# Transposes of q and k in the first attention block: from TensorE to a trip through HBM and VectorE's 32x32 blocks

## The chip, the cores and the metric

The kernel runs on one core of one Trainium2 chip. The time is device time in microseconds of one execution; 1035.2 us is the median of three runs of the kernel before (1035.12, 1035.2 and 1038.44 us). A profile is one execution recorded by the hardware profiler; that of the kernel before took 1035.85 us, of which 1034.1 us lie between its first and its last instruction (the span). Engines are named as in the profile: PE is the matmul engine (PEld its weight loads), DVE the VectorE, ACT the ScalarE, POOL the GpSimd, SP the SyncE, which here only issues DMAs.

## The reference

One decoder layer over 256 tokens of width 2048, all float32. What matters here is its first attention group:

```
h = rmsnorm(x)
[A.q | A.k | A.v | B.c_q | B.c_kv | B.k_rope] = h @ w_in          # 2048 x 4160
A: 8 heads x 128; rotary on the first 32 channels of q and k
   scores = q k^T * 128^-0.5 + mask (three dilated windows, merged)
   out    = softmax(scores) v
B: latent attention, 8 heads, from c_q, c_kv, k_rope
x = x + rmsnorm(concat(A, B) @ w_out);  x = x + rmsnorm(relu(rmsnorm(x) @ w_up)^2 @ w_down)
```

The three dilated windows of the reference, weighted by their softmax denominators, come to one softmax over 256 keys with a bias that holds the logarithm of how many windows a key lies in; the kernel computes them so.

## The kernel before, in words

The 256 tokens are two blocks of 128 (`b` = 0, 1). A matmul of this kernel in float32r is made of three passes (`hi` by `hi`, `lo` by `hi`, `hi` by `lo`), where ACT writes `hi` as a rounded copy of a weight tile (line 311) and DVE the rest `lo` (line 312). A weight tile `raw` comes by a DMA from SP (line 195); five `raw` and eight `hi`/`lo` buffers let this work run some six tiles ahead of PE. One tile of a 512 wide projection feeds 12 matmuls of 512 columns (two k blocks, two token blocks, three passes).

The order of every engine's instructions is written by the program itself: a small planner (`Flow`) holds a clock that each matmul moves on by its estimated cost, and chains (Python generators) that are resumed when the clock has passed the delay that they last yielded. What a chain issues goes into the queues between the matmuls of the projection that runs just then. Engines work through their queues in order, and semaphores are added by the framework, so a chain that is resumed too early makes its engine wait, and whatever stands behind it on that engine.

The first attention group runs in two halves of four heads. For half 0 one projection gives q and k together (`acc_qk`, 192 matmuls), then v (`acc_v`, 96). For half 1 there are three projections of 96 matmuls each: `acc_q`, `acc_k`, `acc_v`. Behind each projection a chain `evac_a` scales the PSUM sums into an SBUF tile `q`, `k` or `v` of 128 tokens x 512 channels per token block (ACT, line 675; the scale `rstd_pre` comes from POOL, line 506), and turns the first 32 channels of each head of q and k by their rotary tables (`rope`, DVE, lines 615 to 618).

When the three chains of a half have ended, `heads_a` starts the four heads in two chains of two heads (0, 1 and 2, 3). For a head it has four PE transposes of 128x128 (q and k, two token blocks; `qkT_a`, line 305) into one PSUM bank, a DVE copy of 128x512 out of it (line 661), then two score matmuls (`sc_a`, line 301), and then `softmax_pv`: bias and maximum on DVE (line 626), exponentials on ACT (line 632), normalising on DVE (lines 635 and 637), three PE transposes of the probabilities (`pT_a`) with an ACT copy (line 643), and the product with v (`o_a`), which ACT and DVE split into the `hi` and `lo` parts of `mixT` (lines 311 and 312). The heads of half 0 run between the matmuls of half 1's projections, those of half 1 between the matmuls of the two projections that follow, `acc_ckv` (192 matmuls of 288 columns) and `acc_cq` (96 of 512).

PSUM has eight banks: four for projections, two for transposes (`tp_bank`, taken in turn by `qkT_a`, `pT_a`, `ckvt` and all later ones), and two for attention (`at_bank`, taken in turn by `sc_a` and `o_a`). Behind `acc_ckv` the chain `latent` transposes the latent `ckv` in two steps of four transposes (`ckvt`), each of which ACT and DVE split out of its bank (lines 315 and 316).

Later in the kernel the result of the up projection is transposed by a trip through HBM and VectorE already: a DMA from ACT's queue writes it out in rows of 512 bytes (`rkeep`, line 965), another reads it back (line 978), and DVE transposes 32x32 blocks (line 980).

Of the kernel before, what the change touches and what calls it, by code (L numbers as in the profile page):

```python
# [18 lines left out]
F32 = mybir.dt.float32  # L19
# [3 lines left out]
AF = mybir.ActivationFunctionType  # L23
# [3 lines left out]
P = 128  # L27
D = 2048
S = 256
NB = S // P  # L30
# [5 lines left out]
RA = 32  # L36
# [51 lines left out]
DA = (3.0, 0.5, 3.0, 3.0, 4.0, 3.0, 0.5)  # L88
# [40 lines left out]
MM = 512 / 2400 + 0.0025  # L129
# [139 lines left out]
def layer(nc, tc, io):  # L269
    flow = Flow()  # L270
# [8 lines left out]
    dram = tc.alloc_tile_pool(name="dram", bufs=1, space=bass.MemoryType.DRAM)  # L279
# [13 lines left out]
    def tp_bank(name):  # L293
        return next_bank(4, 2, name)
# [5 lines left out]
    def mm(out, a, b, start, stop, cost=MM):  # L300
        nc.tensor.matmul(out, a, b, start=start, stop=stop)  # L301
        flow.spend(cost)

    def transpose(out, a):
        nc.tensor.transpose(out, a, ident)
        flow.spend(TR)
# [140 lines left out]
    for c in range(2):  # L447
        wide_d.append([])
        for what, k in DOWN_STEPS[c]:
            if what == "k":  # L450
                ts = [weights.plan(down_weight(c, k), 1, CW)]
            else:
                q, parts_q, back = [lambda c=c, k=k, f=f: f(c, k) for f in (down_sums, down_split, down_back)]
# [57 lines left out]
    pa = pool("pa", "right")  # L511
# [50 lines left out]
    rstd0 = []  # L562
# [19 lines left out]
    def tables():  # L582

        yield D_TAB[0]
        nc.scalar.dma_start(out=pos_i, in_=io["pos"])
        nc.scalar.dma_start(out=cst, in_=io["consts"])
        yield D_TAB[1]
        pos_f = con.tile([P, NB], F32, name="pos_f")
        nc.vector.tensor_copy(pos_f, pos_i)
        ang = pa.tile([P, 2, NB, 96], F32, tag="qkT", bufs=2, name="ang")  # L590
        kk_ = pa.tile([P, 2, NB, 96], F32, tag="qkT", bufs=2, name="kk_")
        for w in range(2):
            for b in range(NB):
                nc.vector.tensor_scalar_mul(ang[:, w, b, :], freq[:, w * 96:(w + 1) * 96], pos_f[:, b:b + 1])
            nc.vector.tensor_scalar(kk_[:, w], ang[:, w], 1.0 / (2 * np.pi), 0.25 * w, op0=OP.mult, op1=OP.add)
        yield 1.0
        nc.vector.tensor_scalar(kk_, kk_, MAGIC, -MAGIC, op0=OP.add, op1=OP.add)
        for c in (C1, C2, C3):
            nc.vector.scalar_tensor_tensor(out=ang, in0=kk_, scalar=-c, in1=ang, op0=OP.mult, op1=OP.add)
        yield 1.0  # L600
        nc.vector.tensor_scalar_add(ang[:, 1], ang[:, 1], float(np.pi / 2))
        nc.vector.tensor_scalar(ang, ang, PI_LO, -PI_LO, op0=OP.min, op1=OP.max)
        yield 4.0
        nc.scalar.activation(trig, ang, AF.Sin)
# [43 lines left out]
        split(mixT[0][:, head, :], mixT[1][:, head, :], o[:, :S])  # L648


    def heads_a(qkv, half, hs, after):
        while any(c in flow.chains for c in after):
            yield 0.5
        for h in hs:
            nm = f"a{half}{h}"
            tp = tp_bank(f"qkT_{nm}")
            for i, w in enumerate("qk"):
                for b in range(NB):
                    transpose(tp[:, (2 * i + b) * P:(2 * i + b + 1) * P], qkv[w][:, b, h * 128:(h + 1) * 128])
            qkT = pa.tile([P, 512], F32, tag="qkT", bufs=2, name=f"qkT_{nm}")  # L660
            nc.vector.tensor_copy(qkT, tp)
            yield DA[0]
            sc = at_bank(f"sc_{nm}")
            mm(sc[:, 0:128], qkT[:, 0:128], qkT[:, 256:384], True, True, MM)
            mm(sc[:, 128:384], qkT[:, 128:256], qkT[:, 256:512], True, True, 2 * MM)
            yield DA[1]
            yield from softmax_pv(pa, DA, sc, bias_a, SCALE_A,
                                  [qkv["v"][:, b, h * 128:(h + 1) * 128] for b in range(NB)], half * 4 + h, nm)
            yield DA[6]

    def evac_a(t, accs, nm, half):
        while pre in flow.chains:
            yield 0.5
        for b in range(NB):
            nc.scalar.activation(t[:, b, :], accs[b][0], AF.Copy, scale=rstd0[0][:, b:b + 1])
        yield 1.0
        while tab in flow.chains:
            yield 0.5
        if nm != "v":
            tv = t.rearrange("p b (h d) -> p b h d", d=128)[:, :, :, :RA]  # L680
            rope(pa, tv, tv, RA // 2, 4, 0, f"{nm}{half}")

    pre = flow.start(prelude())
    tab = flow.start(tables())
# [1 line left out]
    for half in range(2):  # L686
        qkv = {}
        for nms in (("qk", "v") if not half else "qkv"):
            accs = [acc for _, _, acc in proj(xT, [ch_a[half, nms]], f"{nms}{half}",
                                              bank_of=at_bank if (half, nms) == (0, "v") else None)]  # L690
            for i, nm in enumerate(nms):
                t = pa.tile([P, NB, 512], F32, tag=nm, name=f"{nm}_{half}")
                qkv[nm] = t
                evacs.append(flow.start(evac_a(t, [[acc[i]] for acc in accs], nm, half)))
            flow.pump()
        flow.finish(*heads)
        heads = [flow.start(heads_a(qkv, half, hs, evacs), 2.0 + d) for hs, d in (((0, 1), 0.0), ((2, 3), D_PAIR))]
# [58 lines left out]
    kT = pb.tile([P, HB, S], F32, name="kT")  # L756
# [634 lines left out]
```

## Time and profile before

| | |
|---|---|
| median of 3 runs | 1035.2 us |
| the profiled execution | 1035.85 us, span 1034.1 us |
| PE busy | 1022.4 us (99%) |
| DVE, ACT, POOL busy | 834.4 us (81%), 634.6 us (61%), 63.5 us (6%) |
| mean DMA rate | 245 GB/s |
| granted TensorE clock | 0.997 |

Busy time says how much an engine does, the chain of work that ended last says which engine the end waited for. In rows of the timeline and of the chain the first number is the start in us from the span's start and the second the time taken; xN is the number of instructions in the row. In groups, the numbers behind the bar are the busy time in us and the mean ns of one instruction. In rows of DMA issues the last number is the median time in us from the issue to the landing of the data.

### The profile page before, as it was taken

To read this page: it belongs to the slowest core of one execution; us is meant where nothing else is said; L and a number is where in the kernel's file an instruction comes from. 1 tells how busy PE (TensorE), PEld (TensorE's weight loads), DVE (VectorE), ACT (ScalarE), POOL (GpSimd) and SP (SyncE) were. 2 spreads that over 40 slices of the span, in tenths; PEclk is the share of its full clock that TensorE was granted. 3 is DMA by queue.
4 is the path that set the end of the run, shared out by engine and by line. 5 is a ranking of instruction groups with operands and counts; after the bars stand their busy time and mean duration, and the time that the engine had idled before them with its cause. 6 is when DMAs were issued, how large, how long until landed. Compare 5 with 4: busy or idle time off the path is not lost.

```text
span 1034.1 us, 13262 instructions
## 1 busy us (share of the span) xinstructions
PE 1022.4 (99%) x4718; PEld 851.3 (82%) x4718; DVE 834.4 (81%) x1125; ACT 634.6 (61%) x850; POOL 63.5 (6%) x100
## 2 busy tenths in 40 slices
PE   9999999999999999999999999999999999999996
PEld 6888889889888878888888888888888888888885
DVE  6675536577547669999999999898999999899795
ACT  6585536566446467666775767666666665767571
POOL 0000000000001010000100100000101000211100
PEclk9999999999999999999999999999999999999998
DMA  8975447554438478877989887589989867888962
GB/s 288 361 237 166 138 136 223 155 163 144 144 122 263 142 276 284 272 239 258 285 258 302 269 262 258 191 275 335 354 267 366 299 240 258 302 314 303 329 240 82
DMA packets 105298, 253.44 MB, mean 245 GB/s; under 512 B 8720, under 2 KB 29712, under 8 KB 104848
## 3 DMA queue, kind: packets, MB, share of 16 engines
q1 hardware_dynamic: 65744, 175.14, 50.8%
q0 software_dynamic: 16112, 57.68, 16.8%
q10 hardware_dynamic: 23376, 19.78, 6.1%
q8 instruction: 37, 0.61, 0.2%
q14 instruction: 29, 0.24, 0.1%
HBM read 224.78 MB, written 27.79 MB: 244 GB/s over the span
## 4 chain that ended last, share of the span: by engine, by line
PE 96%; DVE 1%; DMA 1%; issue 1%; ACT 0%; POOL 0%; DVEq 0%; POOLq 0%; SPq 0%; ACTq 0%
PE acc_u L301 26%; PE y L301 25%; PE acc_o L301 8%; PE md L301 6%; PE m L301 6%; PE acc_v L301 4%; PE acc_qk L301 4%; PE acc_ckv L301 2%; PE acc_ukv L301 2%; PE acc_q L301 2%; PE acc_cq L301 2%; PE acc_k L301 2%; PE acc_uq L301 2%; PE sc_b L301 1%; DMA raw<-in_w_in 1%
## 5 line engine op out<-in xcount | busy, mean ns | idle before, releaser
L312 DVE TENSOR_TENSOR lo<-raw,hi 128x1024 fp32r<-128x1024 f32 (+3 forms) x207 | 234.1, 1149 | 83.9 <-ACT hi L311 82.5
L311 ACT ACTIVATE hi<-raw 128x1024 fp32r<-128x1024 f32 (+3 forms) x207 | 203.4, 996 | 70.9 <-DMA raw<-in_w_in 16.8
L301 PE MATMUL acc_u<-hi,hT_lo 128*128 128x512 f32 x386 | 150.3, 389 | 0.4 <-DVE hT_lo L312 0.4
L301 PE MATMUL acc_u<-hi,hT_hi 128*128 128x512 f32 x386 | 150.7, 390 | 0.0
L301 PE MATMUL acc_u<-lo,hT_hi 128*128 128x512 f32 x386 | 150.2, 389 | 0.0
L301 PE MATMUL y<-hi,uhi 128*128 128x512 f32 x358 | 139.3, 389 | 0.0
L301 PE MATMUL y<-lo,uhi 128*128 128x512 f32 x358 | 139.3, 389 | 0.0
L301 PE MATMUL y<-hi,ulo 128*128 128x512 f32 x358 | 139.3, 389 | 0.0
L315 ACT ACTIVATE hi<-raw,gcol 128x1024 fp32r<-128x1024 f32 x86 | 97.0, 1148 | 33.1 <-PE acc_u L301 18.2
L316 DVE SCALAR_TENSOR_TENSOR lo<-raw,gcol,hi 128x1024 fp32r<-128x1024 f32 x86 | 106.7, 1273 | 9.4 <-ACT hi L315 9.3
L301 PEld LDWEIGHTS acc_u<-hi,hT_lo 128*128 128x128 f32 x386 | 72.5, 188 | 15.9 <-DVE hT_lo L312 0.8
L301 PEld LDWEIGHTS acc_u<-lo,hT_hi 128*128 128x128 f32 x386 | 72.5, 188 | 14.9
L301 PEld LDWEIGHTS acc_u<-hi,hT_hi 128*128 128x128 f32 x386 | 72.5, 188 | 14.7
L301 PEld LDWEIGHTS y<-hi,uhi 128*128 128x128 f32 x358 | 67.2, 188 | 14.1
L301 PEld LDWEIGHTS y<-lo,uhi 128*128 128x128 f32 x358 | 67.2, 188 | 13.9
L301 PEld LDWEIGHTS y<-hi,ulo 128*128 128x128 f32 x358 | 67.2, 188 | 13.9
L312 DVE TENSOR_TENSOR lo<-st_down,hi 128x1024 fp32r<-128x1024 f32 x46 | 55.0, 1219 | 0.6 <-ACT hi L311 0.6
L301 PE MATMUL acc_o<-hi,mixT_hi 128*128 128x512 f32 x128 | 51.8, 405 | 0.0
L311 ACT ACTIVATE hi<-u 128x1024 fp32r<-128x1024 f32 (+1 forms) x33 | 32.2, 979 | 29.7 <-PE acc_u L301 11.7
L301 PE MATMUL acc_o<-hi,mixT_lo 128*128 128x512 f32 x128 | 50.2, 392 | 0.0
L301 PE MATMUL acc_o<-lo,mixT_hi 128*128 128x512 f32 x128 | 50.0, 390 | 0.0
L311 ACT ACTIVATE hi<-st_down 128x1024 fp32r<-128x1024 f32 x46 | 47.8, 1049 | 3.5 <-DVE st_down L371 2.1
(338 smaller groups left out, 2018.9 us busy)
## 6 DMA issues: line engine op xcount, KB each, us to landing
raw<-in_w_up SPq DMA_DIRECT2D x86, 512.0 KB, 4.8
raw<-in_w_down SPq DMA_DIRECT2D x82, 512.0 KB, 6.1
raw<-in_w_in SPq DMA_DIRECT2D x55, 512.0 KB, 5.1
ab<-in_w_up POOLq DMA_DIRECT2D x17, 1024.0 KB, 7.4
raw<-in_w_out SPq DMA_DIRECT2D x32, 512.0 KB, 4.4
ab_down<-in_w_down POOLq DMA_DIRECT2D x11, 1024.0 KB, 8.9
ulo<-ukeep POOLq DMA_DIRECT2D x20, 512.0 KB, 6.4
rkeep<-r ACTq DMA_DIRECT2D x28, 256.0 KB, 3.4
```

The lines of the kernel that those rows point to most:

```text
L301: nc.tensor.matmul(out, a, b, start=start, stop=stop)
L311: nc.scalar.activation(hi, src, AF.Copy)
L312: nc.vector.tensor_tensor(out=lo, in0=src, in1=hi.bitcast(F32), op=OP.subtract)
L315: nc.scalar.activation(hi, src, AF.Copy, scale=g)
L316: nc.vector.scalar_tensor_tensor(out=lo, in0=src, scalar=g, in1=hi.bitcast(F32), op0=OP.mult, op1=OP.subtract)
```

## The change

The transposes `qkT_a` and the copies out of PSUM are gone. The tiles `q` and `k` get a third block of 512 columns: the projection is now evacuated into blocks 1 and 2, with the channels reordered so that channels 0 to 31 of the four heads come first, then channels 32 to 63, and so on (`a h c` in place of `h a c`). Behind the rotary step, `evac_a` issues from POOL two DMAs that write the two blocks to HBM in rows of 512 bytes (`keep`), after 5 us of the planner's clock two that read them back, and after 8 us more DVE transposes each block in 32x32 pieces (`nc.vector.transpose`), from block 1 to block 0 and from block 2 to block 1. Blocks 0 and 1 then hold the channels of each head on the partitions and the tokens along the row, so the score matmuls read them in place. The tile of half 1 is not taken before the four heads of half 0 have issued their scores (`scored`). The tables' two scratch tiles move to another tag.

```
-            tp = tp_bank(f"qkT_{nm}")
-            for i, w in enumerate("qk"):
-                for b in range(NB):
-                    transpose(tp[:, (2 * i + b) * P:(2 * i + b + 1) * P], qkv[w][:, b, h * 128:(h + 1) * 128])
-            qkT = pa.tile([P, 512], F32, tag="qkT", bufs=2, name=f"qkT_{nm}")
-            nc.vector.tensor_copy(qkT, tp)
-            yield DA[0]
+            qT, kT = [qkv[w][:, :2, h * P:(h + 1) * P] for w in "qk"]
             sc = at_bank(f"sc_{nm}")
-            mm(sc[:, 0:128], qkT[:, 0:128], qkT[:, 256:384], True, True, MM)
-            mm(sc[:, 128:384], qkT[:, 128:256], qkT[:, 256:512], True, True, 2 * MM)
+            scored.append(nm)
+            mm(sc[:, 0:128], qT[:, 0], kT[:, 0], True, True, MM)
+            mm(sc[:, 128:384], qT[:, 1], kT, True, True, 2 * MM)
...
         for b in range(NB):
-            nc.scalar.activation(t[:, b, :], accs[b][0], AF.Copy, scale=rstd0[0][:, b:b + 1])
+            out, a = t[:, b + (nm != "v"), :], accs[b][0]
+            if nm != "v":
+                out, a = [v.rearrange(f"p ({o}) -> p a h c", a=4, h=4) for v, o in ((out, "a h c"), (a, "h a c"))]
+            nc.scalar.activation(out, a, AF.Copy, scale=rstd0[0][:, b:b + 1])
         yield 1.0
         while tab in flow.chains:
             yield 0.5
-        if nm != "v":
-            tv = t.rearrange("p b (h d) -> p b h d", d=128)[:, :, :, :RA]
-            rope(pa, tv, tv, RA // 2, 4, 0, f"{nm}{half}")
+        if nm == "v":
+            return
+        tv = t[:, 1:, :128].rearrange("p b (h d) -> p b h d", d=RA)
+        rope(pa, tv, tv, RA // 2, 4, 0, f"{nm}{half}")
+        keeps = [dram.tile([P, 512], F32, name=f"keep{nm}{half}{b}") for b in range(NB)]
+        yield 2.0
+        for b in range(NB):
+            nc.gpsimd.dma_start(out=keeps[b].rearrange("(a t) (q c) -> (t q) a c", a=4, q=4),
+                                in_=t[:, b + 1, :].rearrange("m (a c) -> m a c", a=4))
+        yield 5.0
+        for b in range(NB):
+            nc.gpsimd.dma_start(out=t[:, b + 1, :], in_=keeps[b])
+        yield 8.0
+        for b in range(NB):
+            nc.vector.transpose(t[:, b, :].rearrange("p (h t q) -> p h q t", h=4, q=4),
+                                t[:, b + 1, :].rearrange("p (q h c) -> p h q c", q=4, h=4))
+            yield 1.0
...
             for i, nm in enumerate(nms):
-                t = pa.tile([P, NB, 512], F32, tag=nm, name=f"{nm}_{half}")
+                flow.until(lambda: len(scored) == 4 * half)
+                t = pa.tile([P, NB + (nm != "v"), 512], F32, tag=nm, name=f"{nm}_{half}")
```

The planner moves the work of this part. All differences of order lie between the rotary step of half 0 and the end of `acc_cq`; behind it the queues of PE, DVE, ACT and SP have the same order in both kernels.

On PE, the first scores of half 0 stand in the projection `acc_q`. Before, one head's scores follow behind 24 of its 96 matmuls, with the transposes of the next head ahead of them:

```order
L301 MATMUL acc_q_0_1_0_706<-lo_594,xT_hi 128x512
L301 MATMUL acc_q_0_1_0_706<-hi_593,xT_lo 128x512
L305 MATMUL qkT_a_750<-ident,q_524 128x128 x2
L305 MATMUL qkT_a_750<-ident,k_525 128x128 x2
L301 MATMUL sc_a_757<-qkT_a_730 128x128
L301 MATMUL sc_a_757<-qkT_a_730 128x256
L301 MATMUL acc_q_0_0_0_705<-hi_632,xT_hi 128x512
```

In the changed kernel:

```order
L301 MATMUL acc_q_0_1_0_718<-lo_637,xT_hi 128x512
L301 MATMUL acc_q_0_1_0_718<-hi_636,xT_lo 128x512
L301 MATMUL sc_a_777<-k_525,q_524 128x128
L301 MATMUL sc_a_777<-k_525,q_524 128x256
L301 MATMUL sc_a_780<-k_525,q_524 128x128
L301 MATMUL sc_a_780<-k_525,q_524 128x256
L301 MATMUL acc_q_0_0_0_717<-hi_658,xT_hi 128x512
```

The scores of heads 0 and 2 now stand together, behind 36 matmuls of `acc_q`.

On DVE, the same stretch, from the fifth `lo` behind the rotary step of k, reads as follows before:

```order
L312 TENSOR_TENSOR lo_710<-raw_707,hi_709 128x1024
L661 COPY qkT_a_730<-qkT_a_725 128x512
L312 TENSOR_TENSOR lo_735<-raw_732,hi_734 128x1024
L661 COPY qkT_a_755<-qkT_a_750 128x512
L626 ISA s_a_760,st_a_761<-sc_a_757,cst 128x128
```

In the changed kernel:

```order
L312 TENSOR_TENSOR lo_722<-raw_719,hi_721 128x1024
L312 TENSOR_TENSOR lo_740<-raw_737,hi_739 128x1024
L693 STREAM_TRANSPOSE q_524<-q_524 128x4x4x32
L693 STREAM_TRANSPOSE k_525<-k_525 128x4x4x32
L312 TENSOR_TENSOR lo_760<-raw_757,hi_759 128x1024
L693 STREAM_TRANSPOSE q_524<-q_524 128x4x4x32
L693 STREAM_TRANSPOSE k_525<-k_525 128x4x4x32
L626 ISA s_a_783,st_a_784<-sc_a_777,cst 128x128
```

Two transposes of the first token blocks, a weight tile's `lo`, and two of the second token blocks stand ahead of the first softmax step, all in DVE's one queue.

On PE, at the end of the same projection, the changed kernel has:

```order
L301 MATMUL o_a_905<-pT_a_888,v_714 128x256
L301 MATMUL o_a_905<-pT_a_888,v_714 128x128
L301 MATMUL o_a_910<-pT_a_894,v_714 128x256
L301 MATMUL o_a_910<-pT_a_894,v_714 128x128
L301 MATMUL sc_a_915<-k_525,q_524 128x128
L301 MATMUL sc_a_915<-k_525,q_524 128x256
L301 MATMUL sc_a_918<-k_525,q_524 128x128
L301 MATMUL sc_a_918<-k_525,q_524 128x256
```

Here `sc_a_915` takes the bank of `o_a_905`, and only `o_a_910` stands between them; before, the other head's product, eight transposes and nine matmuls of `acc_q` stood between these two.

On PE, in `acc_cq`, the two transpose steps of the latent stood one behind the other in the turn of the two transpose banks before:

```order
L305 MATMUL ckvt_1709<-ident,ckv 128x128 x4
L301 MATMUL acc_cq_1_0_1675<-hi_1517,xT_hi 128x512
L301 MATMUL acc_cq_1_0_1675<-lo_1518,xT_hi 128x512
L301 MATMUL acc_cq_1_0_1675<-hi_1517,xT_lo 128x512
L305 MATMUL ckvt_1721<-ident,ckv 128x128 x4
```

In the changed kernel:

```order
L305 MATMUL ckvt_1696<-ident,ckv 128x128 x4
L305 MATMUL pT_a_1705<-ident,s_a_1546 128x128 x3
L301 MATMUL acc_cq_0_0_1665<-hi_1553,xT_hi 128x512
L301 MATMUL acc_cq_0_0_1665<-lo_1554,xT_hi 128x512
L301 MATMUL acc_cq_0_0_1665<-hi_1553,xT_lo 128x512
L305 MATMUL ckvt_1720<-ident,ckv 128x128 x4
```

A `pT_a` has moved between them and takes the other bank, so both `ckvt` steps now use the same bank.

More of the change, by code (lines that the diff above doesn't have):

```diff
@@ L589, in tables @@
         nc.vector.tensor_copy(pos_f, pos_i)
-        ang = pa.tile([P, 2, NB, 96], F32, tag="qkT", bufs=2, name="ang")
-        kk_ = pa.tile([P, 2, NB, 96], F32, tag="qkT", bufs=2, name="kk_")
+        ang = pa.tile([P, 2, NB, 96], F32, tag="s", bufs=2, name="ang")
+        kk_ = pa.tile([P, 2, NB, 96], F32, tag="s", bufs=2, name="kk_")
         for w in range(2):
@@ L648, in softmax_pv @@
         split(mixT[0][:, head, :], mixT[1][:, head, :], o[:, :S])
+    scored = []
     def heads_a(qkv, half, hs, after):
```

## The prediction

> **What bounds the kernel now.** I read the page's busy times and chain first, then the chain in order of time around the change.
>
> ```profile
> PE 1022.4 (99%) x4718; PEld 851.3 (82%) x4718; DVE 834.4 (81%) x1125; ACT 634.6 (61%) x850; POOL 63.5 (6%) x100
> PE 96%; DVE 1%; DMA 1%; issue 1%; ACT 0%; POOL 0%; DVEq 0%; POOLq 0%; SPq 0%; ACTq 0%
> ```
>
> PE is busy 99% of the span and holds 96% of the chain: whatever PE no longer does is won, and each us for which PE waits is lost. The stretch that the change touches, in order of time:
>
> ```profile
> 50.95 21.76 PE acc_v L301 x96
> 72.72 2.73 PE acc_q L301 x12
> 75.44 0.44 PE qkT_a L305 x4
> 75.88 2.76 PE acc_q L301 x12
> ...
> 79.08 0.66 PE sc_a L301 x4
> ...
> 91.36 0.33 PE pT_a L305 x3
> ...
> 94.82 0.65 PE o_a L301 x4
> ...
> 100.43 0.69 PE acc_k L301 x3
> ```
>
> The rows follow each other without a gap: from 72.72 us, where half 1's projections begin, to 203.51 us, where `acc_cq` ends, PE never stands still.
>
> ```profile
> 72.72:203.51 130.79, 130.79 (x705) 113.72 (x705) 74.23 (x142) 67.02 (x117) 0.70 (x1) 1.00 0.58 175
> ```
>
> Over these 130.79 us PE is busy 130.79, DVE 74.23 and ACT 67.02, the clock is granted in full, and the DMA engines are busy 0.58 of the time. Here DVE, ACT and DMA have room, PE has none.
>
> **The change part by part.** *Removed.*
>
> ```profile
> L305 PE MATMUL qkT_a<-ident,q x16: 270/272/273, 75.3 to 175.9; 128*128 128x128 f32 x16
> L661 DVE COPY qkT_a<-qkT_a x8: 678/692/692, 75.9 to 176.5; 128x512 f32<-128x512 f32 x8
> ```
>
> There are 16 transposes of q and as many of k, 8 groups of four. On the chain a group takes 0.44 us (row at 75.44), since the 0.272 us of one overlap with the next. Gain: 8 x 0.44 = **3.5 us**. The chain also has some 20 fewer changes between kinds of matmul. The rows at 72.72 and 75.88 have 12 matmuls in 2.73 and 2.76 us, where 96 undisturbed take 21.76, or 0.2267 each and 2.72 for 12; at 0.01 to 0.04 each (an estimate from these rows) that is 0.2 to 0.8 us, which I leave to the low end.
>
> In the Trainium skill, "VectorE: DVE Perf Modes", section "Rules for kernel authors", says to transpose 128x128 on TensorE wherever PSUM will do as the destination; it speaks against this change. "TensorE: Matmul & The Clock Gate", section "PE-mode transpose", gives some 275 ns for one in a kernel; the row's 272 ns agrees. The gain by that figure would be 32 x 0.275 = 8.8 us.
>
> The 8 copies leave DVE and 8 block transposes join it. The nearest rows:
>
> ```profile
> L980 DVE STREAM_TRANSPOSE uT<-c 128x512 f32<-128x512 f32 x16 | 10.8, 694 | 0.0
> 66.96 0.28 DVE L616 TENSOR_TENSOR rp_q<-q,trig 128x128 f32<-128x128 f32 x1
> ```
>
> The same operation on 128x512 takes 0.69 us, but writes its elements side by side; the new one writes them four apart. As an upper bound I take four pieces of 128 columns at 0.28 us, 1.12 us. I take 1.1, because of the spread writes. DVE's load grows by 8 x 0.4 = 3.3 us of its 56 idle ones: nothing, unless it stands in the one place below.
>
> In the Trainium skill, "Vector Engine (DVE) Microarchitecture Reference", section 5.2, "Measured stream behaviour on trn2", gives 1.05 ns per column for adjacent words and 1.71 to 2.51 where the output hops at each element. By that 0.69 us would become 1.03 to 1.44 (an estimate from that page); no row of this trace shows it.
>
> *Added: the round trip.* Each half stores four times 256 KB and loads them back, 4.2 MB in all, on DMA engines that are 0.58 busy. The price is latency, and only half 0 is tight. When can the DMAs start?
>
> ```profile
> 67.48 0.42 DVE L618 TENSOR_TENSOR q<-rp_q,rp_q 128x256 f32<-128x256 f32 x1
> 68.87 0.42 DVE L618 TENSOR_TENSOR k<-rp_k,rp_k 128x256 f32<-128x256 f32 x1
> 69.22 4.62 DVE L312 TENSOR_TENSOR lo<-raw,hi 128x1024 fp32r<-128x1024 f32 x4
> 74.42 1.22 DVE L312 TENSOR_TENSOR lo<-raw,hi 128x1024 fp32r<-128x1024 f32 x1 [0.58 <-ACT hi L311]
> 76.52 1.06 ACT L311 ACTIVATE hi<-raw 128x1024 fp32r<-128x1024 f32 x1 [0.96 <-DMA raw<-in_w_in]
> ```
>
> q is ready at 67.90, k at 69.29. POOL stands idle since `rstd_pre`, so its eight DMAs wait for nothing else, but they wait for each other. What they cost:
>
> ```profile
> L379 POOL DMA_DIRECT2D ab<-in_w_up x17 | 12.2, 718 | 215.1 <-DVE lo L312 185.4 <-DMA raw<-in_w_up 29.7
> L1036 POOL DMA_DIRECT2D ulo<-ukeep x20 | 10.8, 540 | 180.0 <-PE y L301 93.8 <-DVE st_down L371 85.5 <-issue 0.7
> L965 ACTq DMA_DIRECT2D rkeep<-r x28: 366/369/389, 402.0 to 662.5; - x28
> rkeep<-r ACTq DMA_DIRECT2D x28, 256.0 KB, 3.4
> c<-rkeep ACTq DMA_DIRECT2D x28, 256.0 KB, 4.9
> DMA to landing us min/median/max: 2.3/4.7/13.2
> ukeep<-uT POOLq DMA_DIRECT2D x8, 256.0 KB, 7.7
> ulo<-ukeep POOLq DMA_DIRECT2D x20, 512.0 KB, 6.4
> ```
>
> POOL needs 0.54 us to issue 128 rows and 0.72 for 256, so 0.54 + 3 x 0.18 = 1.08 us for 512 pieces (an estimate). The stores are issued at 67.9, 69.0, 70.05 and 71.1. `rkeep` has the same shape and size and lands 3.4 us after a 0.37 us issue; with POOL's longer issue 4.1. Loads as `c<-rkeep`, 4.9. So q's two blocks land at 72.2 + 4.9 = 77.1 (POOL is free at 72.2) and 69.0 + 4.1 + 4.9 = 78.0, k's at 79.05 and 80.1. DVE's queue then runs (order rows above): `lo` to 75.64, the next `lo` to 76.86, q at 77.1 to 78.2, k at 79.05 to 80.15, the `lo` whose `hi` is ready at 77.58 to 81.4, q to 82.5, k to 83.6. PE arrives at 72.72 + 36 x 0.2267 = 80.88. The first score matmul (0.22 us) needs the first blocks and finds them; the second, at 81.1, waits until 83.6: **2.5 us lost**. Low bound: 3.4 for a store and 2.3 for a load, the least landing of this tile, with 0.69 a transpose: DVE is through at 80.84, no wait. High bound: the POOL rows, 7.7 and 6.4 (the first adds into HBM, the second is twice the size): k lands at 71.1 + 7.7 + 6.4 = 85.2, its first block at 84.15, DVE is through at 88.7, a wait of 7.6. I take the middle, since shape and size are those of `rkeep`. Behind the waiting transpose on DVE stand `lo` tiles; the one between the pairs is first used by `acc_k`, near 100.43 us, so some 18 us cover it.
>
> In half 1 the trip of k runs under `acc_v` (21.76 us) and takes some 12 us by the same steps. Its last block transpose stands behind seven `lo` in DVE's queue, which keep PE's pace of 2.7 us a tile, so it ends at 19 of the 24 us that `acc_v` and 18 matmuls of `acc_ckv` give: no price.
>
> *Moved: two banks.* At the end of `acc_q`, `sc_a` needs the bank of an `o_a` that only one other `o_a` (0.65 us) separates from it.
>
> ```profile
> 95.51 0.38 ACT L311 ACTIVATE mixT_hi<-o_a 128x256 fp32r<-128x256 f32 x1 [0.87 <-PE o_a L301]
> 95.92 0.42 DVE L312 TENSOR_TENSOR mixT_lo<-o_a,mixT_hi 128x256 fp32r<-128x256 f32 x1 [1.50 <-ACT mixT_hi L311]
> ```
>
> `o_a` ends at 95.47, its bank is free at 96.34, 0.87 later. **0.25 us lost** (bounds 0 and 0.9, if nothing covers it). Likewise `ckvt`: both steps now use one bank, and the first must be split out by ACT and DVE. The trace shows this with `cqt`, which PE ends at 206.24 + 0.44 = 206.68:
>
> ```profile
> 206.24 0.44 PE cqt L305 x4
> 206.71 0.48 ACT L315 ACTIVATE cqT_hi<-cqt,gcol 128x256 fp32r<-128x256 f32 x1 [0.16 <-PE cqt L305]
> 207.74 0.47 ACT L315 ACTIVATE cqT_hi<-cqt,gcol 128x256 fp32r<-128x256 f32 x1 [0.55 <-DVE cqT_lo L316]
> 208.25 0.48 DVE L316 SCALAR_TENSOR_TENSOR cqT_lo<-cqt,gcol,cqT_hi 128x256 fp32r<-128x256 f32 x1 [0.54 <-ACT cqT_hi L315]
> ```
>
> ACT and DVE take turns and end at 208.73, 2.05 us later. PE has `pT_a` (0.33) and three matmuls (0.68) to fill it: **1.0 us lost** (bounds 0, and 1.5 if ACT comes to it late).
>
> *Sum.* -3.5 + 2.5 + 0.25 + 1.0 = +0.25 us on the profiled execution's 1035.85, 1036.1. That execution lies 0.65 above the median of the runs; against 1035.2 the forecast is **1035.5 us**, no change.
>
> **The rivals.** A measurement of this kernel tells about 0.3%, 3.1 us, from no change.
>
> (1) *The trip is hidden.* If DVE is through by 81.1, the sum is -3.5 + 1.25 = -2.25: 1032.9. For it: DMA is 0.58 busy, so landings could lie at the low bound. Against it: eight POOL DMAs in a row, and a strided write. Only if the bank waits vanish too and the saved changes of kind add up to 0.8 does it reach -4.3, 1030.9, faster.
>
> (2) *A transpose costs PE its full 0.272 us*, the duration in its row. Then 32 x 0.272 = 8.7 us go, and the sum is -8.7 + 3.75 = -4.95: 1030.2. Against it: the chain has the next matmul 0.44 us behind four of them. (The Trainium skill's 275 ns of "PE-mode transpose", above, would say the same 8.7 to 8.8 us.)
>
> (3) *The trip is as slow as POOL's present DMAs.* The sum is -3.5 + 7.6 + 1.25 = +5.35: 1040.6, slower. It decides once the last block transpose of half 0 ends after 86.4 us (81.1 + 3.1 + 3.5 - 1.25). For it: these are POOL's DMAs, the only rows of that queue of 256 to 512 KB say 6.4 and 7.7, and the loads wait in one queue behind four stores. Against it: the add and the larger size in those rows.
>
> (4) *DVE's wait starves the weights.* Every us that DVE is held beyond about 98 us costs one; landings would have to take 15 us more. No row says so.
>
> That the change leaves transposes on PE is excluded by the order: no `qkT_a` row is left.
>
> **How the numbers follow.** The forecast, a sum between 1033.5 and 1038.3, has 0.46; (1) with its bank waits 0.22, still within 0.3%; (1) without them 0.08 and (2) 0.04, faster; (3) 0.19 and (4) 0.01, slower. So 0.12 faster, 0.68 same, 0.20 slower. The full bounds are -4.3 and 7.6 + 0.9 + 1.5 - 3.5 = +6.5, 1030.9 to 1041.7; leaving a tenth out on each side gives 1032.0 to 1039.2.
>
> **What would show it.** Right: no `qkT_a`, and PE's busy pieces between 72.72 us and the end of `acc_cq` 3.5 us shorter; a gap of 2 to 3 us on PE ahead of the second `sc_a` near 81 us, released by a DVE transpose, whose own idle time is put down to the loads of `k`; small gaps ahead of the third `sc_a` and the second `ckvt`; block transposes near 1.1 us. Wrong: no gap near 81 us (1), one over 5 us (3), PE waiting for `lo` (4), or landings of the stores nearer 7.7 than 4.1. A time outside 1032.0 to 1039.2 would mean that a wait stands somewhere I have not looked.

## The result: 1041.2 us, slower by half a per cent, and the profile after

| | before | after |
|---|---|---|
| median, lowest and highest of 8 runs each | 1035.7 us (1034.4 to 1038.4) | 1041.2 us (1037.8 to 1043.4) |
| the profiled execution, its span | 1035.85, 1034.1 us | 1041.69, 1039.8 us |
| from the start of `acc_q` to the end of `acc_cq` | 130.79 us | 136.70 us |

The ratio is 1.0048 with a 95% interval of 1.0030 to 1.0066, some 5 us. The forecast was 1035.5, the range 1032.0 to 1039.2: the time lies above it. The whole loss stands in the stretch that the prediction looked at, 5.9 us of it. The first two rows are from the page of the changed kernel (busy times, and the shares of the chain of waits), the third is the row of that stretch, read as the one before:

```profile
PE 1022.6 (98%) x4686; PEld 850.0 (82%) x4686; DVE 837.0 (80%) x1125; ACT 634.3 (61%) x850; POOL 74.4 (7%) x116
PE 86%; DMA 6%; DVE 4%; ACT 2%; issue 2%; POOL 0%; SPq 0%; DVEq 0%; POOLq 0%; ACTq 0%
71.41:208.11 136.70, 130.35 (x673) 112.28 (x672) 77.13 (x142) 67.25 (x117) 7.60 (x12) 0.98 0.61 196
```

PE held 96% of the chain before and holds 86% now; most of the rest runs through DMAs and DVE. PE stands still for 6.35 of the 136.70 us, and a new number is in the row: the granted clock is 0.98 and no longer 1.00. The chain around the first scores, in order of time:

```profile
68.12 0.76 POOL keepq L686
68.87 5.39 DMA keepk<-k
74.27 0.28 issue
74.55 6.14 DMA k<-keepk
...
81.72 0.58 DVE lo L312
82.31 0.54 issue
82.85 1.08 DVE q L693
83.93 0.91 DVE k L693
84.84 0.04 issue
84.88 2.50 PE sc_a L301 x6
87.39 12.95 PE acc_q L301 x51
```

It reads: k's first token block goes out at 68.87 us, takes 5.39 us into HBM and 6.14 us back, and behind its transpose DVE has three more steps (a weight tile's `lo`, the second block of q and that of k) before PE can go on to the second score matmul. On PE itself (timeline, then its waits from 60 to 230 us as total, number, longest):

```profile
82.03 0.46 PE L301 MATMUL sc_a<-k,q 128*128 128x128 f32 x2 [2.50 <-DVE k L693]
84.88 2.50 PE L301 MATMUL sc_a<-k,q 128*128 128x256 f32 x6 [2.40 <-DVE k L693]
```

```profile
PE sc_a L301 <- DVE k L693: 4.9, 2, 2.5
PE ckvt L305 <- DVE mixT_lo L316: 1.2, 1, 1.2
PE sc_a L301 <- DVE mixT_lo L312: 0.3, 1, 0.3
```

PE waits at the first score matmul, 2.50 us, as well as at the second, 2.40 us. The prediction had the second alone. What follows these waits is slower too. In the table by stretches the last three numbers of a row are granted clock, DMA share and GB/s:

```profile
82.00:84.00 2.00, 0.46 (x2) 0.29 (x2) 2.00 (x3) 1.46 (x2) 0.00 (x0) 0.83 0.88 311
84.00:86.00 2.00, 1.12 (x3) 0.94 (x4) 0.83 (x1) 0.88 (x1) 0.00 (x0) 0.50 0.87 253
86.00:88.00 2.00, 2.00 (x7) 1.67 (x6) 1.39 (x9) 0.98 (x4) 0.00 (x0) 0.50 0.07 25
88.00:90.00 2.00, 2.00 (x6) 1.57 (x5) 1.97 (x5) 0.99 (x5) 0.00 (x0) 0.50 0.00 0
90.00:92.00 2.00, 2.00 (x9) 1.58 (x9) 0.54 (x1) 0.44 (x1) 0.00 (x0) 0.96 0.68 185
```

From about 83 to 90 us TensorE runs at half its clock. The eight score matmuls take 0.46 + 2.50 = 2.96 us, and the 51 matmuls of `acc_q` behind them 12.95. Without the waits (the first experiment below) the same rows take 1.31 and 11.61 us, so 1.65 + 1.34 = 3.0 us are lost behind the waits, on top of them.

Not all of that is the clock. The row from 82 us has a clock of 0.83, so only its last 0.7 us are at half speed. The first pair of scores ran ahead of that, from 82.03 us, and still took 0.46 us where the pair takes 0.22 in a stream without a wait (e4_filled below). In e8_act_store, where the clock stays at 1.00, the six score matmuls behind a wait take 1.35 us, where they take 1.09 in the stream. So each start behind a wait costs some 0.25 us, two of them 0.5. The clock's own share is 2.50 - 1.35 = 1.15 on the scores and 1.34 on `acc_q`, together 2.5 us. Now the stretch adds up: -3.5 for the transposes, +4.9 for the two waits, +0.5 for the two starts, +2.5 for the clock, +0.3 and +1.2 at the two banks, together +5.9.

DVE's block transposes, the two of k in half 0 in the timeline and all of q's as a group (duration in ns, least, median and most):

```profile
80.78 1.10 DVE L693 STREAM_TRANSPOSE k<-k 128x512 f32<-128x512 f32 x1 [2.71 <-DMA k<-keepk]
...
83.77 1.06 DVE L693 STREAM_TRANSPOSE k<-k 128x512 f32<-128x512 f32 x1
```

```profile
L693 DVE STREAM_TRANSPOSE q<-q x4: 1070/1082/1098, 77.0 to 125.4; 128x512 f32<-128x512 f32 x4
```

The granted clock of a whole execution differs between the runs of this kernel: 0.997 in three of the eight, with 1037.8 to 1039.8 us, and 0.994 or 0.995 in five, with 1040.8 to 1043.4. So the slow clock does not follow in every execution.

### The profile page after: what moved, and what is told of

Read it like the earlier page. It is cut to its first block, busy times and chain, and to the rows that moved or that the text cites. A ratio compares the mean times of both kernels' runs of the same rounds, so it can differ in the third digit from the quotient of the medians.

```text
span 1039.8 us, 13245 instructions
## 1 busy us (share of the span) xinstructions
PE 1022.6 (98%) x4686; PEld 850.0 (82%) x4686; DVE 837.0 (80%) x1125; ACT 634.3 (61%) x850; POOL 74.4 (7%) x116
## 4 chain that ended last, share of the span: by engine, by line
PE 86%; DMA 6%; DVE 4%; ACT 2%; issue 2%; POOL 0%; SPq 0%; DVEq 0%; POOLq 0%; ACTq 0%
PE acc_u L301 26%; PE y L301 23%; PE acc_o L301 8%; PE m L301 5%; PE md L301 5%; DMA raw<-in_w_in 3%; PE acc_ckv L301 2%; PE acc_ukv L301 2%; PE acc_k L301 2%; PE acc_v L301 2%; PE acc_cq L301 2%; PE acc_uq L301 2%; DVE lo L312 2%; DMA ab_down<-in_w_down 1%; PE acc_q L301 1%
```

## The experiments

**Theory A**: half 0's trip lands later than reckoned, PE waits for it at two matmuls, and the idle time costs the clock as well; half 1's trip costs nothing. **Rival B**: the new order of PE's work costs the time, whatever the trip does. **Rival C**: the added DMAs slow down others (the weights) in both halves. The column "stretch" is how much longer than before the profiled execution takes from the first matmul of `acc_q` to the end of `acc_cq` (before: 130.96 us, reckoned from the first matmul's own start); what lies around the stretch takes 902.1 to 904.4 us in the thirteen profiled executions, so their whole spans tell less than the stretch. "Waits" are PE's waits for block transposes, "clock" the lowest granted clock in any 2 us of 74 to 92 us. The kernel before had medians of 1036.3 us beside e1, e2, e4 and e5, of 1035.8 beside e6, e7, e9 and e10, and of 1035.7 beside e3, e8 and e11.

| kernel | median (range) us | ratio to before, 95% interval | stretch us | waits us | clock |
|---|---|---|---|---|---|
| the change | 1041.2 (1037.8 to 1043.4) | 1.0048 (1.0030 to 1.0066) | +5.9 | 2.5 + 2.4 | 0.50 |
| e1_no_trip | 1034.9 (1033.3 to 1036.0) | 0.9985 (0.9976 to 0.9993) | -2.0 | none | 1.00 |
| e2_half1 | 1035.5 (1034.7 to 1039.9) | 0.9997 (0.9986 to 1.0008) | -0.4 | none | 1.00 |
| e3_half0 | 1042.5 (1041.8 to 1043.2) | 1.0059 (1.0041 to 1.0076) | +6.5 | 5.5 in two | 0.50 |
| e4_filled | 1039.9 (1039.3 to 1041.3) | 1.0030 (1.0020 to 1.0041) | +2.9 | none (filled) | 1.00 |
| e6_fill_first | 1039.6 (1038.7 to 1044.6) | 1.0034 (1.0020 to 1.0048) | +2.6 | 1.8 | 1.00 |
| e7_fill_second | 1040.8 (1037.6 to 1042.7) | 1.0037 (1.0021 to 1.0052) | +4.8 | 2.4 | 0.50 |
| e9_long_rows | 1040.1 (1039.1 to 1041.3) | 1.0038 (1.0025 to 1.0051) | +4.4 | 3.3 in two | 0.50 |
| e11_light | 1039.9 (1038.1 to 1041.9) | 1.0037 (1.0020 to 1.0054) | +3.1 | 2.9 in two | 0.50 |
| e8_act_store | 1037.6 (1036.5 to 1040.3) | 1.0015 (1.0004 to 1.0026) | -0.3 | 1.4 | 1.00 |
| e5_later | 1033.0 (1032.5 to 1035.1) | 0.9966 (0.9953 to 0.9978) | -2.3 | none | 1.00 |
| e10_apart | 1032.0 (1031.5 to 1033.5) | 0.9961 (0.9949 to 0.9973) | -3.7 | none | 1.00 |

### Is it the trip, and which half's?

**e1_no_trip** keeps the order of the matmuls and takes the trip away (no DMAs and no block transposes; the scores are of untransposed blocks).

```
-            qT, kT = [qkv[w][:, :2, h * P:(h + 1) * P] for w in "qk"]
+            qT, kT = [qkv[w][:, 1:, h * P:(h + 1) * P] for w in "qk"]
...
-            nc.gpsimd.dma_start(out=keeps[b]..., in_=t[:, b + 1, :]...)
...
-            nc.gpsimd.dma_start(out=t[:, b + 1, :], in_=keeps[b])
...
-            nc.vector.transpose(t[:, b, :]..., t[:, b + 1, :]...)
```

> Leaves out the two DMAs of each trip and the block transposes, so the scores are made of q and k that are not transposed; order and everything else as in the changed kernel. Theory A (the profile of the changed kernel: PE waits 2.5 + 2.4 us for the block transposes of half 0, after that its granted clock is halved for some 6.7 us, which costs 3.0 more; two waits for a bank cost 0.3 and 1.2; the transposes taken from PE give 3.5): no wait for DVE, full clock, -3.5 + 1.5 = -2.0 us against before. Theory B (the loss is not the trip's lateness but the new order of PE's work, its bank waits and broken runs): still +5 to +6. If a transpose costs PE its full 0.27 us: -8.7 + 1.5 = -7.

Measured: 0.9985, and 2.0 us less in the stretch, which is -3.5 + 0.3 + 1.2. The chain around the first scores has no wait:

```profile
80.38 1.31 PE sc_a L301 x8
81.69 11.61 PE acc_q L301 x51
```

B falls: the new order alone does not lose. The transposes are worth the 3.5 us of the chain's 0.44 us for four, and not 8.7 us.

**e2_half1** and **e3_half0** each make the trip in one half, and leave the other half its PE transposes and copies:

```
+            if half == TRIP:
                 qT, kT = [qkv[w][:, :2, h * P:(h + 1) * P] for w in "qk"]
+            else:
+                tp = tp_bank(f"qkT_{nm}")
+                ... (four transposes and the copy, as before)
```

> Only half 1 makes the trip, half 0 has its PE transposes and copies again. Theory A: four groups of PE transposes less (-1.75), the wait at the second ckvt stays (+1.2), no wait for a block transpose, full clock: -0.5 us. Theory C (the loss is contention: the trip's traffic and POOL's DMAs make weights late, in both halves alike): about half of the loss, +2 to +3 us.

> The trip in half 0 alone; half 1 has its PE transposes and copies as before. From the change's own terms: 1.75 us won (four groups of transposes), 4.9 us waited at the first two scores, 0.3 at a bank, and 1.2 at the second ckvt if both still share a bank, so 3.5 to 4.7 us above the kernel before where the clock holds, and up to 7.7 where it is halved behind the waits. Should half 1's trip be what costs, it is no slower than the kernel before.

Measured: half 1 alone -0.4 us in the stretch (half of the 3.5 us won, 1.2 lost at `ckvt`) and no difference in time; half 0 alone +6.5. Together that is +6.1, where the change has +5.9. PE's waits in e3_half0:

```profile
PE sc_a L301 <- DVE k L707: 5.5, 2, 3.5
PE sc_a L301 <- DVE mixT_lo L312: 0.3, 1, 0.3
```

C falls: half 1's trip moves as many bytes and costs nothing. It also shows that the wait at the second `ckvt` belongs to half 1's order of work, since it is in e2_half1 and not here.

### Is the clock a cost of its own?

**e4_filled** gives PE idle matmuls in place of the idle time, ahead of both waiting score matmuls; **e6_fill_first** and **e7_fill_second** ahead of one of them:

```
+            if (half, h) == (0, 0):
+                for _ in range(15):
+                    nc.tensor.matmul(sc[:, 128:512], zero[:, :P], zero[:, :384], start=True, stop=True)
             mm(sc[:, 0:128], qT[:, 0], kT[:, 0], True, True, MM)
+            if (half, h) == (0, 0):
+                for _ in range(15):
+                    nc.tensor.matmul(sc[:, 128:512], zero[:, :P], zero[:, :384], start=True, stop=True)
             mm(sc[:, 128:384], qT[:, 1], kT, True, True, 2 * MM)
```

> The changed kernel, with 15 idle bf16 matmuls of 384 columns (some 0.16 us each, 2.4 us) ahead of each of the first two score matmuls of half 0, written to a part of the bank that the scores then overwrite or that is never read. They last about as long as PE waits there. Theory A: the waits are filled, not shortened, so the time of the waits stays (4.9), but PE is not idle and the clock stays full: 3.0 us less than the changed kernel, +2.5 to +3 against before, granted clock 0.997. If the low clock does not come from PE's idle time: clock as before at 0.994 to 0.995, and +5.5 or more.

> The change with 15 idle matmuls of 384 columns (bf16 zeros, overwritten by the score) ahead of the first score matmul of half 0 alone: PE then waits only once, some 2.4 us, at the second score matmul. If the granted clock falls only because the two waits (2.50 and 2.40 us, 0.46 us of work between them) lie so close together, it stays at full speed and the time is that of the kernel with both waits filled, 1039 to 1040 us, 3 us above the kernel before. If one wait of 2.4 us is enough, the rows behind the scores are slow again (acc_q x51 in 12.9 us and not 11.6), and the time is that of the change, some 5.5 us above the kernel before.

> The same with the 15 idle matmuls ahead of the second score matmul of half 0 alone: PE waits once, 2.5 us, at the first score matmul, and has work from there on. Only the pair of waits halves the clock: 3 us above the kernel before, acc_q x51 in 11.6 us. One wait is enough: 5.5 us above it, with the slow rows now at the idle matmuls (over 4 us in place of 2.45) and behind them.

With both filled, the chain has, and the table by stretches shows:

```profile
80.89 2.45 PE sc_a L663 x15
83.34 0.22 PE sc_a L301 x2
83.56 2.44 PE sc_a L667 x15
86.00 1.09 PE sc_a L301 x6
87.09 11.61 PE acc_q L301 x51
```

```profile
84.00:86.00 2.00, 2.00 (x14) 1.30 (x12) 1.38 (x2) 1.07 (x1) 0.00 (x0) 1.00 0.89 263
```

The trip is as late as before, PE loses the same 4.9 us (2.45 + 2.44, on matmuls whose results are overwritten), and yet the stretch is 3.0 us shorter than the change's, 2.9 instead of 5.9. So the 3.0 us, the clock and the two starts, come from PE standing still. In e6_fill_first one wait of 1.8 us is left, and the clock holds in the profiled execution (51 matmuls in 11.57 us); of its nine runs one, of 1044.6 us, has a mean clock of 0.994, and two have 0.996. Its median of 1039.6 us is what was expected where the clock holds, but its wait was not the 2.4 us that was to be tested. In e7_fill_second one wait of 2.4 us is left, and the clock falls behind it:

```profile
83.73 0.46 PE L301 MATMUL sc_a<-k,q 128*128 128x128 f32 x2 [2.37 <-DVE k L696]
84.03 4.28 PE L664 MATMUL sc_a<-zero 128*128 128x384 bf16 x15
```

```profile
84.00:86.00 2.00, 2.00 (x11) 1.04 (x10) 2.00 (x3) 1.88 (x2) 0.00 (x0) 0.66 1.12 358
86.00:88.00 2.00, 2.00 (x8) 0.99 (x7) 0.54 (x1) 0.46 (x1) 0.00 (x0) 0.50 0.68 239
88.00:90.00 2.00, 2.00 (x12) 1.78 (x11) 1.19 (x8) 0.34 (x2) 0.00 (x0) 0.98 0.03 12
```

The 15 idle matmuls take 4.1 us in its chain instead of 2.45. But the mean clock is 0.994 or 0.995 in only two of its seven runs and 0.997 or 0.998 in the other five. So neither expectation for e7_fill_second held as written: a single wait of 2.4 us can be enough, and isn't always. The Trainium skill, "TensorE: Matmul & The Clock Gate", section "What's actually happening", says that the gate judges PE's activity in a window of 3413 ns that runs freely, so that the moment of a change differs between runs; that fits the scatter, which no run here can trace to it. The length of the window is in the traces. Where a 2 us row lies at 0.50 in part, its mean tells for how long: the clock is halved for 0.68 + 2 + 2 + 2 + 0.16 = 6.8 us in the change, and for 1.36 + 2 + 0.08 = 3.4 us here; in the same way it is 6.8 us in e3_half0 and e9_long_rows and 3.4 in e11_light, once or twice that window in all five. The same page of the Trainium skill asks, in the table of "Why this matters for your kernels", for no idle gap of more than about 3 us; here 2.4 us alone, and 2.5 and 2.4 with 0.46 us of work between, halved the clock, so by its letter the rule would not have priced this change.

### Why is the trip late?

From the end of k's rotary step to the landing of its first block, the prediction had 9.8 us (69.29 to 79.05). The change took 12.7 (67.97 to 80.69). The other profiled executions in which the trip is the change's own (e3_half0, e6_fill_first and e7_fill_second) took 12.3 to 12.7. Three experiments were each meant to take one suspect away; in e11_light that did not succeed.

**e9_long_rows** writes the stores in rows of 2 KB:

```
-            nc.gpsimd.dma_start(out=keeps[b].rearrange("(a t) (q c) -> (t q) a c", a=4, q=4),
-                                in_=t[:, b + 1, :].rearrange("m (a c) -> m a c", a=4))
+            nc.gpsimd.dma_start(out=keeps[b], in_=t[:, b + 1, :])
```

> The change with the stores written in straight rows of 2 KB (128 pieces in place of 512 per store); it leaves out the reordering of the rows in HBM, so the scores are of misplaced data, with the same instructions otherwise. If the many short pieces make the trip late, a store's issue falls from 0.75 to 0.94 us to some 0.55 as for the loads, its landing from 5.4 us to below 4, the waits at the first two scores come to under 2.5 us in all, the clock holds, and the time is within 1 us of the kernel before. If the DMA engines are late because they are full with the weights at that time (share 1.01 to 1.04 from 70 to 82 us), only the issue is shorter: waits of 4 us or more, and a time 4 to 5.5 us above the kernel before.

**e11_light** loads half of the bytes of the weight tiles that come in these microseconds:

```
+        if name in ["raw%d" % i for i in range(28, 36)]:
+            out, src = out[:, :1], src[:, :1]
         self.nc.sync.dma_start(out=out, in_=src)
...
+                if 28 <= i < 36:
+                    self.split_fn(v(hi), v(lo), raw[:, :512].unsqueeze(1).to_broadcast([P, 2, 512]), g)
```

> The change with eight weight tiles (those that come while half 0's trip runs, 66 to 90 us) loaded by half and the half used twice: 2 MB less in that stretch, every other instruction the same; it leaves out half of the rows of these weights, so the projection of half 1's q is of other weights. If the trip is late because its DMAs share the DMA engines with the weights, the landings of k's first block fall from 5.4 (store) and 6.1 us (load) towards the 4.2 and 4.0 us that the same DMAs of half 1 take at a DMA share of 0.6, the waits at the first two scores fall from 4.9 us to 2.5 or less, the clock holds, and the time is within 1.5 us of the kernel before. If the trip's own chain (POOL's issues in one queue, four stores and four loads at once) makes it late, the landings stay above 5 us, the waits above 4 us, and the time 4 to 5.5 us above the kernel before.

**e8_act_store** issues the stores from ACT:

```
-            nc.gpsimd.dma_start(out=keeps[b].rearrange("(a t) (q c) -> (t q) a c", a=4, q=4),
+            nc.scalar.dma_start(out=keeps[b].rearrange("(a t) (q c) -> (t q) a c", a=4, q=4),
```

> The change with the stores issued from ACT's queue in place of POOL's. ACT issued the stores of rkeep, of the same shape, in 0.37 us where POOL takes 0.75 to 0.94, so the fourth store leaves 1 to 1.5 us earlier if ACT stands ready; it waits for the rotary step with its weight copies behind it. If POOL's issue is what is late, the waits at the first two scores fall from 4.9 to 3 us and the time lies 1 to 3 us above the kernel before. If the DMA engines are full, what leaves earlier lands no earlier: waits of 4 us or more and 4 to 5.5 us above it.

The waits of the first two ended between their expectations; their times lie 4.2 us above the kernel before, as the second expectation of each had it. In the chain of e9_long_rows, and then of e11_light:

```profile
68.23 4.23 DMA keepk<-k
...
72.75 6.31 DMA k<-keepk
```

```profile
69.40 4.23 DMA keepk<-k
...
73.91 5.45 DMA k<-keepk
```

Either edit brings the store from 5.4 to 4.2 us (5.3 to 5.6 in the executions with the change's own trip), and in e11_light the load takes 5.5 (5.7 to 6.1 in the same). From the end of k's rotary step to the landing it is 11.4 and 10.9 us. The waits shrink from 4.9 to 3.3 and 2.9 us, but one of the two is still 2.4, the clock still falls, and the times hardly improve.

e11_light did not make the DMA engines light, though. While the loads run they are as full as in the change and move as many bytes (share, then GB/s, at the end of a row). The change first, then e11_light:

```profile
74.00:78.00 4.00, 4.00 (x19) 3.31 (x18) 2.55 (x3) 1.19 (x2) 1.08 (x2) 1.00 1.01 371
```

```profile
74.00:78.00 4.00, 4.00 (x20) 3.30 (x19) 3.21 (x3) 1.80 (x3) 0.99 (x2) 1.00 1.01 367
```

So what the trip would take beside few weights is not tested in half 0. The store issued from ACT does more. The first row is DVE's timeline, the second PE's, with its only wait for a block transpose, the third and fourth are the issues of 60 to 78 us:

```profile
77.27 1.09 DVE L693 STREAM_TRANSPOSE k<-k 128x512 f32<-128x512 f32 x1
```

```profile
81.36 1.35 PE L301 MATMUL sc_a<-k,q 128*128 128x256 f32 x6 [1.43 <-DVE k L693]
```

```profile
keepk<-k ACTq DMA_DIRECT2D x2, 256.0 KB, 4.1
k<-keepk POOLq DMA_DIRECT2D x2, 256.0 KB, 5.8
```

k's first block is transposed from 77.27 us, 9.7 us after the end of its rotary step (67.55 us), so it has landed by then: the prediction's 9.8 us. The edit moves the stores to another queue, shortens their issue, and leaves no store ahead of the loads on POOL; which of these counts was not taken apart. PE finds it at the first score matmul and waits 1.4 us at the second, the clock holds in the profiled execution, and the stretch is 0.3 us shorter than before (-3.5 + 0.3 + 1.2 + 1.4 + 0.3 for the start behind the wait). Over 11 runs it is 1.0015 of the kernel before (0.4 to 2.7 us slower), more than this one execution says; three of its runs have a mean clock of 0.995 or 0.996 and 1038.1 to 1040.3 us.

For the DMA engines' load there is only a comparison of the halves of the change itself: in the lighter stretch of half 1 (share 0.59 from 130 to 145 us) the same DMAs land in about 4 us, as they were reckoned. The first row is for that stretch, the next two are its issues; the last one is half 0's load, from 60 to 78 us:

```profile
130.00:145.00 15.00, 15.00 (x68) 12.43 (x67) 7.08 (x11) 6.02 (x8) 2.62 (x4) 1.00 0.59 187
```

```profile
keepk<-k POOLq DMA_DIRECT2D x2, 256.0 KB, 4.2
k<-keepk POOLq DMA_DIRECT2D x2, 256.0 KB, 4.0
```

```profile
k<-keepk POOLq DMA_DIRECT2D x2, 256.0 KB, 6.1
```

The halves differ in more than the share, so this argues for the load and does not show it. So the lateness has no single owner. POOL's queue and the short pieces each take a part, and the queue is the larger; the part of the full DMA engines is argued only. The stores of k issued from ACT landed in 4.1 us although the share was 1.00 from 68 to 74 us.

### What remains of the gain when the scores come later?

**e5_later** starts half 0's heads 13 us of the planner's clock later, behind 72 matmuls of `acc_q` in place of 36, and moves the taking of half 1's tile into its evacuation chain, so that the projections don't stop for it. **e10_apart** adds a longer delay between the latent's two transpose steps.

```
-        heads = [flow.start(heads_a(qkv, half, hs, evacs), 2.0 + d) ...
+        heads = [flow.start(heads_a(qkv, half, hs, evacs), 2.0 + (0.0 if half else 13.0) + d) ...
...
-        while pre in flow.chains:
+        while pre in flow.chains or len(scored) < 4 * half:
             yield 0.5
+        t = qkv[nm] = pa.tile([P, NB + (nm != "v"), 512], F32, tag=nm, name=f"{nm}_{half}")
```

and, for e10_apart, in `latent`:

```
-            yield 1.0
+            yield 4.0 if n == "kv" else 1.0
```

> The changed kernel with the heads of half 0 started 13 us later in the planner's clock, so that the first scores stand behind 72 instead of 36 matmuls of acc_q (8.2 us later), and the tile of half 1 taken in the evacuation's own chain. Theory A: PE comes to the first scores at some 87.7 us, after the last block transpose (84.8): no wait, full clock; -3.5 + 1.2 (the ckvt wait stays) = -2.3 us against before. Theory C: the traffic is the same, so the loss stays at +5.

> The kernel of e5_later (heads of half 0 start 13 us later in the planner) with a longer delay between the two transpose steps of the latent (4.0 in place of 1.0), so that six matmuls of acc_cq and one pT_a with its product stand between them more than before. If the 1.2 us that PE waits ahead of the second ckvt are a loss of the bank alone, the wait goes and the time is 1.2 us below e5_later, 4.7 us below the kernel before. If the wait only moves to the next taker of a bank, it is the time of e5_later.

In the chain of e5_later PE comes to the scores at 87.67 us, past the end of the trip, and goes through them without a wait:

```profile
75.88 11.80 PE acc_q L301 x52
87.67 0.65 PE sc_a L301 x4
```

The stretch is 2.3 us shorter than before (-3.5 + 1.2), and 3.7 in e10_apart, where the wait at the second `ckvt` is gone too and the whole 3.5 us arrives. e10_apart, at 0.9961 of the kernel before (0.9949 to 0.9973, some 4 us faster), beats both kernels; so does e5_later. The 1.2 us between the two show in the stretch; the intervals of their times overlap.

## Why the prediction was wrong, and where it was right

**Right.** The 3.5 us of the removed transposes: e10_apart has no wait for the trip nor at a bank, and 3.7 us less. That rejects rival (2). The block transpose at 1.1 us: 1.06 to 1.10 measured, inside the 1.03 to 1.44 worked out from the Trainium skill's "Vector Engine (DVE) Microarchitecture Reference", section 5.2. The bank of `o_a`, 0.25 forecast and 0.3 measured; the bank of `ckvt`, 1.0 and 1.2. No price in half 1.

**Luck.** The wait at the second score matmul was 2.5 forecast and 2.40 measured. The forecast was for all that DVE lags behind PE, and 2.50 us of that lag had already been waited for at the first score matmul.

**Wrong: "The first score matmul needs the first blocks and finds them."** It waited 2.50 us. The step behind this is the landing of the trip: a store was put at 4.1 us and a load at 4.9, and k's first block took 5.39 and 6.14. The prediction moved `rkeep`'s 3.4 us from ACT's queue to POOL's and added only the longer issue, which it even put too high (1.08 us where the trace now shows 0.75 to 0.94 per store). e8_act_store, where the stores do come from ACT's queue, comes nearest to its numbers: the stores of k land in 4.1 us and the first block is there in time, though the loads take 5.8 and not 4.9. And it judged the DMA engines by their mean of 0.58 over 130 us. Where the loads lie they were already full; the kernel before has, in the microseconds of the stores and of the loads:

```profile
70.00:74.00 4.00, 4.00 (x19) 3.30 (x19) 3.84 (x4) 3.39 (x5) 0.00 (x0) 1.00 0.56 173
74.00:78.00 4.00, 4.00 (x21) 3.31 (x20) 3.05 (x3) 2.92 (x4) 0.00 (x0) 1.00 1.02 368
```

Share 1.02 at 368 GB/s from 74 us, before a byte of the trip was added. In the change it is 1.02 from 70 us on, with the stores. Against PE's arrival DVE is through 5.3 us later (84.84 against 79.53), where 2.7 were reckoned (83.6 against 80.88). This missed 2.4 of the 5.7 us between the sum (+0.25) and the measured +5.9.

**Wrong by omission: the clock.** No term says what an idle PE costs beyond the idle time. It was 3.0 us, the larger half of the miss: 2.5 for the clock and 0.5 for the two starts. The sum with the measured waits but without these, -3.5 + 4.9 + 0.3 + 1.2 = +2.9, is the stretch that e4_filled measures, and on 1035.2 us it comes to 1038.1, inside the range. The Trainium skill's "TensorE: Matmul & The Clock Gate", which the prediction cites for a transpose, has the rule about idle gaps.

**The range.** The full bounds, 1030.9 to 1041.7, hold the measured 1041.2. A tenth of their width left out on each side would give 1032.0 to 1040.6; how 1039.2 was reached isn't worked out. The low bound's 2.3 us is the least of stores and loads of `rkeep` together; the loads alone take 2.7 at least, which changes no wait.

**Rival (3)**, a trip as slow as POOL's present DMAs, came near in time (1040.6) for a partly other reason. By its own condition, the last block transpose ending 5.5 us after PE's arrival, it had not quite been reached (5.3), and it forecast a loss from the wait alone; without the clock the kernel would have lost 3.4 us. **Rival (4)** did not occur: no `lo` is among PE's waits.

## What to carry to other kernels

Take the time of an added transfer from rows of the same queue at the same DMA load, and read that load in the few microseconds where the transfer will lie, not over the stage, with the transfer's own bytes on top. Where a matmul may come to wait more than about 2 us, price what follows the wait as well as the wait; here the clock added 2.5 us and starting again 0.5 to 4.9. And a change that trades work of the bottleneck engine for latency needs its consumer moved by that latency in the same edit: the same trip that lost 5 us gained 3 once the scores stood 36 matmuls later.

## What the runs showed of the hardware that was not expected

- The granted TensorE clock fell to 0.50 with idle times of 2.4 us, or of 2.9 to 5.5 us in two parts, during the wait or within 1 us behind it, and stayed at 1.00 behind single ones of 1.4 and 1.8 us, each in one profiled execution. It stayed low for 3.4 us (e7_fill_second, e11_light) or 6.8 us (the change, e3_half0, e9_long_rows), and for no other length in these five. Between executions of one kernel it differs: 0.994 or 0.995 over the whole time in five of the change's eight runs, in all five of e3_half0, in two of seven of e7_fill_second and in none of e4_filled.
- Idle matmuls that are overwritten keep the clock up. They bring the change 3.0 us in the stretch, 2.5 of it the clock, while PE loses the same time to the trip.
- A matmul group behind a wait takes some 0.25 us longer than in a stream, at the full clock: 0.46 for 0.22 us (two score matmuls, the change), 1.35 for 1.09 (six, e6_fill_first and e8_act_store).
- A 256 KB store of 512 pieces of 512 bytes took POOL 0.75 to 0.94 us to issue, 128 rows of 2 KB 0.54 to 0.73 (two in 1.07 to 1.28 us), and ACT, with 512 pieces again, 0.37 to 0.52.
- The same load of 256 KB from HBM landed in 4.0 us (k, half 1) at a DMA share of 0.59, in 5.2 (q, half 1) at 0.81, and in 6.1 and 6.8 (k and q, half 0) at 1.0.
